# One trunk step with mLSTM and band attention: whole conditioning rows at the start, another order in the first MLP's last group, and head groups one after the other in attention

## The chip, the cores and the metric

The kernel runs on one core of a Trainium2 chip. The metric is the device time of one execution in microseconds (us). TensorE (PE) multiplies matrices, VectorE (DVE) and ScalarE (ACT) do elementwise work, GpSimd (POOL) a little, and SyncE (SP) issues every DMA. Each engine works through its own queue in order.

## The reference

The step has two layers over 1056 tokens: 1024 of a prompt and 32 of a second sequence, each with its own conditioning vector c. Layer 0 is an mLSTM mixer and an MLP with squared ReLU, layer 1 is band attention (own chunk of 64 tokens and 8 chunks before it, or 512 cached keys for the second sequence) and such an MLP. Ahead of each mixer and each MLP the stream is scaled and shifted by values that come from c:

```python
sh1, sc1, g1, sh2, sc2, g2 = jnp.split(ada_mod(c, p['w_ada'][l], p['b_ada'][l])[:, None, :], 6, axis=-1)
u = x * (1 + sc1) + sh1
...
kv = (x * (1 + kv_scale) + kv_shift) @ p['w_kv']
q = (u @ p['w_q_b'][lb]).reshape(Bsz, S, NH_B, HD_B)
...
y = o @ p['w_out_b'][lb]
x = layer_norm(ALPHA * x + (1 + g1) * y, p['ln_g'][l, 0], p['ln_b'][l, 0])
u = x * (1 + sc2) + sh2
f = jnp.square(jax.nn.relu(u @ p['w_up'][l])) @ p['w_down'][l]
x = layer_norm(ALPHA * x + (1 + g2) * f, p['ln_g'][l, 1], p['ln_b'][l, 1])
```

Here ada_mod is silu(c) @ w + b, the width is 1024 and that of the MLP 4096. All values are 32-bit floats.

## The kernel before

**Products.** The stream lies in SBUF with features on partitions, eight chunks (k = 0 to 7) of 128 features, and in three token blocks TBS: block 0 (tokens 0 to 383), block 1 (384 to 767) and block 2 (768 to 1055, whose last 32 are the second sequence). A product of two fp32 matrices is made of three matmuls on halves that add up to the operand: high by high, high by low, low by high (proj, lines 118 to 120; for v lines 455 to 457). Each operand is therefore split: for weights, a copy on ACT makes the high half and a subtraction on DVE the low one (split, lines 89 and 90); for the scaled stream U (u in layer 1's MLP), modulate makes the high half on ACT (L324), the same value unrounded on DVE or ACT (L326, L328), and the low half on DVE (L329).

**Buffers and order.** Raw weights are loaded into a ring of three buffers (tag raw), their halves lie in six (tag wc); a buffer is used anew when its readers are done. PSUM has eight banks. A scheduler of the framework places each engine's instructions; small generators (Flow) are advanced one step at a tick, and the code says after which product a step is due. In attention PE's order is the code's own (manual_schedule). Each engine then keeps that order, waiting where an operand is missing.

**The start.** The 8 rows (k) of 128 by 2048 of w_ada that give shift and scale of layer 0 are loaded in quarters (q) of 512 columns: first quarters 0 and 2 of all k (ada_start(0)), which hold what chunks 0 to 3 need, later 1 and 3. Two matmuls for each k put their 32 output rows on partitions 32q. Each half ends with copies (sada), transposes (adat) and an addition (ada). x is transposed on PE (xps), U is made from PSUM, and x is copied to xt and stored (xsp). v's product begins with chunks 0 to 3 of block 0, stops for the second half of the conditioning, and goes on; qk follows.

**MLP.** w_up and w_down go in 8 groups g of 512 hidden features. up(g, c, ti) is one product of 128 hidden features c and block ti (24 matmuls), down(g, w, fc, block) one of 128 output features (12 matmuls), added to acc by DVE (add_gated). In the last group g = 7 all ups stand ahead of all downs; then the downs go block by block, and behind each block its layer norm is started: sums on DVE, sr on ACT, mean_n and var_n as matmuls on PE, the new U. In layer 0 q's product comes next, then kv.

**kv and attention.** Ahead of the first kv token block the four blocks of 128 cached keys are loaded, copied twice side by side (kd_c) and transposed (kt_c). uk is the scaled stream for kv. Attention works on units (gp, c): head group pair gp of 2 and chunk c, wide ones (chunks 8 to 15) and slim ones in turn, and the two gp in turn. PE makes scores (s), DVE their maxima (mx), ACT the exponentials (p), PE their transposes (pt, pT) and the sums (pv), which become QO.

**After attention.** open_acc loads the stream back into three accumulators acc, gain_shift scales it (L893, 24 times on ACT), and out_proj (op_b) multiplies QO by w_out's halves w_ob: first output columns pr 0 for blocks 2, 1, 0, then pr 1 to 3. The norms of the blocks are due after so many ticks (W10), and MLP 1 follows.

Of the kernel before, what the change touches and what calls it, by code (L numbers as in the profile page):

```python
# [75 lines left out]
def trunk_kernel(ctx: ExitStack, tc: tile.TileContext, a, o):  # L76
# [116 lines left out]
    def ada_load(k, q, mk):  # L193
        raw = mk([P, 512], f"rada_0_{k}_{q}")
        nc.sync.dma_start(raw, a["w_ada"][0, k * P:(k + 1) * P, q * 512:(q + 1) * 512])
        return raw
    PRE = 3
    pre = {(k, q): ada_load(k, q, wc_tile) for k, q in ((0, 0), (0, 2), (1, 0), (1, 2))[:PRE]}
    c_rows = raw_tile([16, P], "c_rows")
    nc.sync.dma_start(c_rows[0:8], a["c_prompt"].rearrange("b (k p) -> (b k) p", p=P))  # L200
    nc.sync.dma_start(c_rows[8:16], a["c_sample"].rearrange("b (k p) -> (b k) p", p=P))
    tp = tpt("tp_c")
# [128 lines left out]
    START = 5  # L331
# [35 lines left out]
    def x_block(t0, n, load=True):  # L367
        if load:
            x_load(t0, n)
        for k in range(KC):  # L370
            ps = tpt(f"xps_{t0}_{k}")
            for i in range(0, n, P):
                xr = xrows[t0, i]
                m = xr.shape[0]
                nc.tensor.transpose(ps[:, i:i + m], xr[:, k * P:(k + 1) * P], ident[:m, :m])
# [4 lines left out]
            nc.scalar.copy(xt[:, k, t0:t0 + n], ps[:, :n])  # L380
            yield
        nc.sync.dma_start(xsp[0][:, :, t0:t0 + n], xt[:, :, t0:t0 + n])

    start_tile = rot([(raw_tile, 3), (wc_tile, 4), (y_tile, 1), (rc_tile, 1)])

    def ada_start(half):

        ps = adat(f"ada_0{half}")
        for k in range(KC):
            for q in (half, half + 2):  # L390
                raw = pre.pop((k, q), None) or ada_load(k, q, start_tile)
# [18 lines left out]
    for i in range(START):  # L410
        flow.tick()
# [287 lines left out]
    def after_v0(t):  # L699
# [4 lines left out]
        elif t == 5:  # L704
            flow.finish(xa[2])
# [728 lines left out]
```

## Time and profile before

| | us |
|---|---|
| median of three runs (lowest 2531.4, highest 2533.92) | 2532.17 |
| the profiled execution | 2531.46 |
| its span in the profile | 2529.6 |

Places in the trace by PE's rows: the start with v to 86.6, qk, mLSTM and the output gate to 435, op_a to 532, the first MLP to 1279, q to 1380, kv to 1442, attention to 1647, op_b to 1760, the second MLP to 2517. A row of waits names the engine, the line that waited, what it waited for, the total, the times and the longest. In rows of instructions, "out<-in" are the program's names, followed by the shape, and brackets give the idle time just before. A matmul's own time overlaps that of its neighbours: the distance of two starts is what one costs. A row of stretches gives busy time of each engine, the granted share of the PE clock, the mean share of the DMA engines that was busy, and GB/s.

### The profile page before, as it was taken

Reading aid. Unit: us, or ns where it says so; the run is one execution under the profiler, and the core shown is the slowest. Engines: PE = TensorE matmul, PEld = TensorE weight load, DVE = VectorE, ACT = ScalarE, POOL = GpSimd, SP = SyncE. Lnnn points to the kernel's source line nnn. Section 1 sums busy time; section 2 is a strip of 40 time slices with the busy share of each in tenths; the row PEclk is TensorE's granted clock in tenths of the full one; section 3 lists DMA queues with packets and bytes.
Section 4 is the critical chain, followed back from the end, with each engine's and each line's share of the span. In section 5 each row is a group of like instructions: output and inputs, shape, how many; then the busy total and the mean of one; then the engine's idle time right before and its main releaser. Section 6 shows DMA issues by size and latency. Waiting matters only on the chain.

```text
span 2529.6 us, 39897 instructions
## 1 busy us (share of the span) xinstructions
PE 2466.1 (97%) x15784; PEld 2356.0 (93%) x15784; DVE 1677.0 (66%) x3851; ACT 953.2 (38%) x2023; POOL 165.8 (7%) x315
## 2 busy tenths in 40 slices
PE   7999999999999999999999899989999999999998
PEld 3899999999999999999999877689999999999997
DVE  3899998788678678766597677737634334343337
ACT  3654446383212211221376566637621221221222
POOL 0111100000000000000001144400000000000003
PEclk9999999999999999999999999989999999999999
DMA  7522323413224234223123400051111111111101
GB/s 235 166 89 92 95 80 105 152 34 102 90 85 136 81 94 132 87 90 122 59 84 102 101 1 1 6 156 34 51 51 42 51 43 50 42 59 34 51 26 70
DMA packets 192063, 201.20 MB, mean 80 GB/s; under 512 B 9336, under 2 KB 180748, under 8 KB 191876
## 3 DMA queue, kind: packets, MB, share of 16 engines
q1 hardware_dynamic: 191876, 198.65, 25.4%
q8 instruction: 124, 2.03, 0.3%
q14 instruction: 63, 0.52, 0.1%
HBM read 183.38 MB, written 17.60 MB: 79 GB/s over the span
## 4 chain that ended last, share of the span: by engine, by line
PE 83%; DVE 7%; ACT 3%; DMA 3%; issue 1%; SPq 0%; DVEq 0%; POOL 0%; ACTq 0%
PE dn L118 10%; PE dn L120 10%; PE dn L119 10%; PE up L118 10%; PE up L119 9%; PE up L120 9%; PE pv L1284 2%; PE pt L1264 2%; PE s L1234 2%; DVE ada_room L236 1%; PE q L118 1%; PE q L119 1%; PE q L120 1%; DMA ada_room<-in_w_ada_dram 1%; PE op_a L118 1%; PE op_a L119 1%
## 5 line engine op out<-in xcount | busy, mean ns | idle before, releaser
L118 PE MATMUL dn<-h,w_dn 128*128 128x384 f32 (+2 forms) x1568 | 505.9, 323 | 0.0
L120 PE MATMUL dn<-h,w_dn 128*128 128x384 f32 (+2 forms) x1568 | 502.1, 320 | 0.0
L119 PE MATMUL dn<-h,w_dn 128*128 128x384 f32 (+2 forms) x1568 | 497.8, 317 | 0.0
L959 DVE SCALAR_TENSOR_TENSOR acc<-dn,ada,acc 128x384 f32<-128x384 f32 (+5 forms) x536 | 244.0, 476 | 237.2 <-PE dn L120 235.0
L118 PEld LDWEIGHTS dn<-h,w_dn 128*128 128x128 f32 x1568 | 294.5, 188 | 0.8 <-issue 0.2
L119 PEld LDWEIGHTS dn<-h,w_dn 128*128 128x128 f32 x1568 | 294.3, 188 | 0.1
L120 PEld LDWEIGHTS dn<-h,w_dn 128*128 128x128 f32 x1568 | 294.0, 187 | 0.0
L998 DVE TENSOR_TENSOR r<-r 128x384 f32<-128x384 f32 (+1 forms) x192 | 100.0, 523 | 275.6 <-ACT h L997 275.0
L996 ACT ACTIVATE r<-up 128x384 f32<-128x384 f32 (+1 forms) x192 | 88.5, 462 | 448.0 <-PE up L120 437.2
L118 PE MATMUL up<-U,w_up 128*128 128x384 f32 (+1 forms) x768 | 249.3, 325 | 0.0
L119 PE MATMUL up<-U,w_up 128*128 128x384 f32 (+1 forms) x768 | 248.2, 323 | 0.0
L120 PE MATMUL up<-U,w_up 128*128 128x384 f32 (+1 forms) x768 | 247.4, 322 | 0.0
L118 PE MATMUL up<-u,w_up 128*128 128x384 f32 (+1 forms) x768 | 246.5, 321 | 0.0
L120 PE MATMUL up<-u,w_up 128*128 128x384 f32 (+1 forms) x768 | 246.5, 321 | 0.0
L119 PE MATMUL up<-u,w_up 128*128 128x384 f32 (+1 forms) x768 | 246.4, 321 | 0.0
L89 ACT CAST w_up<-raw_up 128x1024 fp32r<-128x1024 f32 x64 | 66.8, 1048 | 413.1 <-PE dn L120 274.3
L236 DVE SCALAR_TENSOR_TENSOR aacc<-rada,cs,aacc 128x256 f32<-128x256 f32 x448 | 190.4, 478 | 0.0
L118 PEld LDWEIGHTS up<-U,w_up 128*128 128x128 f32 x768 | 144.2, 188 | 0.1
L120 PEld LDWEIGHTS up<-U,w_up 128*128 128x128 f32 x768 | 144.3, 188 | 0.0
L120 PEld LDWEIGHTS up<-u,w_up 128*128 128x128 f32 x768 | 144.2, 188 | 0.0
L119 PEld LDWEIGHTS up<-U,w_up 128*128 128x128 f32 x768 | 144.2, 188 | 0.0
L119 PEld LDWEIGHTS up<-u,w_up 128*128 128x128 f32 x768 | 144.1, 188 | 0.0
(318 smaller groups left out, 5260.5 us busy)
## 6 DMA issues: line engine op xcount, KB each, us to landing
raw_up<-in_w_up_dram SPq DMA_DIRECT2D x64, 512.0 KB
raw_dn<-in_w_down_dram SPq DMA_DIRECT2D x64, 512.0 KB
rada<-in_w_ada_dram SPq DMA_DIRECT2D x48, 512.0 KB
ada_room<-in_w_ada_dram SPq DMA_DIRECT2D x32, 512.0 KB
rada<-in_w_ada_dram SPq DMA_DIRECT2D x32, 256.0 KB
rada<-in_w_ada_kv_dram SPq DMA_DIRECT2D x16, 512.0 KB
acc<-xsp SPq DMA_DIRECT2D x4, 1536.0 KB
rc<-rc_d SPq DMA_DIRECT2D x8, 528.0 KB
```

Of the source, the lines that this page charges most:

```text
L89: nc.scalar.copy(dst_h, src)
L118: nc.tensor.matmul(ps, wh, mov(0, k), start=(k == 0), stop=False)
L119: nc.tensor.matmul(ps, wh, mov(1, k), start=False, stop=False)
L120: nc.tensor.matmul(ps, wl, mov(0, k), start=False, stop=(k == nk - 1))
L236: nc.vector.scalar_tensor_tensor(acc[:, cnd], raw[:, k], sc, acc[:, cnd], op0=ALU.mult, op1=ALU.add)
L959: nc.vector.scalar_tensor_tensor(xs, ps[:, off + o:off + o + mm_], gate[:, fc, cnd:cnd + 1], xs, op0=ALU.mult, op1=ALU.add)
L996: nc.scalar.activation(r, ps[:, :n], AF.Relu)
L998: nc.vector.tensor_mul(r, r, r)
L1234: nc.tensor.matmul(s[:, b, :w], qst, kk[i][:, g, k0 + j0:k0 + j0 + w], start=(i == 0), stop=(i == 1))
L1264: nc.tensor.transpose(pt[:kp, j - j0, pr * P:(pr + 1) * P], ps_[pr][:, j * P:j * P + kp], ident)
L1284: nc.tensor.matmul(pv[64 * e:64 * e + 64, :nq], V[:kp, vt0 + j, g * 64:(g + 1) * 64], pts[e][:kp, j, :nq], start=(j == 0), stop=(j == nt - 1))
```

## The change

Five things are done. At the start, whole rows of w_ada are loaded (two DMAs of 128 x 1024 each into one wc buffer), four matmuls for each k fill all 128 output partitions, and the whole conditioning is finished in one step, ahead of v; U is made from xt in SBUF instead of PSUM; v goes chunk by chunk over the three token tiles of a block, with the next block's transposes and U between, and x is stored after v. In the first MLP's last group, three ups (c = 3 of block 1, c = 2 and 3 of block 2) come after block 0's downs, and the weights of the downs are asked for when the first block needs them. The cached keys go in with kv's token blocks 0, 2, 4 and 6. Attention does all units of gp 0 and then all of gp 1; pr 0's two halves of w_out are loaded and split within gp 1. The accumulators are loaded in the order 2, 1, 0, with two halves of pr 1 and of pr 2 after the first two. In W10 two of the due times grow.

```diff
@@ -190,15 +190,19 @@
...
+    def ada_load(k):
+
+        raw = wc_tile([P, 2 * D], f"rada_0_{k}")
+        for i in range(2):
+            nc.sync.dma_start(raw[:, i * D:(i + 1) * D], a["w_ada"][0, k * P:(k + 1) * P, i * D:(i + 1) * D])
         return raw
-    PRE = 3
...
     c_rows = raw_tile([16, P], "c_rows")
...
+    adaw = [ada_load(k) for k in range(4)]
...
@@ -364,54 +356,46 @@
...
+    def x_transpose(t0, n, eng):
+
...
+            eng[k % len(eng)](xt[:, k, t0:t0 + n], ps[:, :n])
+            yield
+
+    def u_chunks(t0, n):
+        for k in range(KC):
             for off, m, cnd in segs(t0, n):
...
-                modulate(ps[:, off:off + m], m, sc1[:, k, cnd:cnd + 1], sh1[:, k, cnd:cnd + 1],
+                modulate(xt[:, k, t0 + off:t0 + off + m], m, sc1[:, k, cnd:cnd + 1], sh1[:, k, cnd:cnd + 1],
                          uap(0, k, t0 + off, m), uap(1, k, t0 + off, m), tmp[:, :m])
...
+    def ada_mm(k):
+
+        for q in range(4):
+            nc.tensor.matmul(ada_ps[32 * q:32 * q + 32, :512], cs[:, k, :], adaw[k][:, q * 512:(q + 1) * 512],
+                             start=(k == 0), stop=(k == KC - 1))
...
+    def ada_first():
+
+        sb = rc_tile([P, 512], "sada")
+        ps2 = nmt("adat")
+        for hf in range(2):
+            (nc.scalar.copy if hf else nc.vector.tensor_copy)(sb[:, 256 * hf:256 * hf + 256],
+                                                              ada_ps[:, 256 * hf:256 * hf + 256])
+            for b in (2 * hf, 2 * hf + 1):
+                nc.tensor.transpose(ps2[:, b * P:(b + 1) * P], sb[:, b * P:(b + 1) * P], ident)
+        nc.vector.tensor_tensor(
+            ada[:, 0:16, :].rearrange("p (q b) j -> p q b j", q=4),
+            ps2.rearrange("p (b q j) -> p q b j", b=4, q=4)[:, :, :, 0:2],
+            pt2[:, 0:16].rearrange("p (q b) -> p q b", q=4)[:, :, :, None].broadcast_to([P, 4, 4, 2]), op=ALU.add)
...
@@ -434,45 +418,57 @@
...
+    def v_chunk(ps, ws, t, k):
+        w = ws[k // 4]
+        n = w.shape[-1]
+        uh, ul = uap(0, k, t * P, P), uap(1, k, t * P, P)
+        nc.tensor.matmul(ps[:, :n], uh, w[:, 0, k % 4, :], start=(k == 0), stop=False)
+        nc.tensor.matmul(ps[:, :n], uh, w[:, 1, k % 4, :], start=False, stop=False)
+        nc.tensor.matmul(ps[:, :n], ul, w[:, 0, k % 4, :], start=False, stop=(k == KC - 1))
...
+    def v_first(ws, nxt):
+
+
+        vts = []
+        for bi, (t0, n) in enumerate(TBS):
+            ts = range(t0 // P, (t0 + n + P - 1) // P)
+            pss = {t: (mmt, nmt, mmt)[bi % 2 * (t % 2)](f"v_0_{t}") for t in ts}
+            for k in range(KC):
+                for t in ts:
+                    v_chunk(pss[t], ws, t, k)
+                nxt(bi, k)
+            vts += [v_out(pss[t], 0, t) for t in ts]
...
@@ -694,36 +690,40 @@
...
+    xT = [x_transpose(t0, n, (nc.scalar.copy, nc.vector.tensor_copy)[:2 - (i > 0)]) for i, (t0, n) in enumerate(TBS)]
+    uT = [u_chunks(t0, n) for t0, n in TBS]
+    x_load(*TBS[0])
+    adaw += [ada_load(k) for k in (4, 5)]
+    for k in range(4):
+        ada_mm(k)
+    vw = [v_weight(0, 0)]
+    adaw += [ada_load(k) for k in (6, 7)]
+    for k in range(4, 6):
+        ada_mm(k)
+    for _ in xT[0]:
+        pass
+    for k in range(6, 8):
+        ada_mm(k)
+    vw.append(v_weight(0, 1))
+    x_load(*TBS[1], wc_tile)
+    x_load(*TBS[2])
+    ada_first()
+    for _ in uT[0]:
+        pass
+    flow.add(small_params(), SP)
+
+    def next_u(bi, k):
+        if bi < 2:
+            next(xT[bi + 1])
+            next(uT[bi + 1])
+            if k == KC - 1:
+                for g in (xT[bi + 1], uT[bi + 1]):
+                    for _ in g:
+                        pass
...
+    vts = [v_first(vw, next_u)]
+    for t0, n in TBS:
+        nc.sync.dma_start(xsp[0][:, :, t0:t0 + n], xt[:, :, t0:t0 + n])
...
@@ -797,15 +797,17 @@
...
-    def open_acc(l, order):
+    def open_acc(l, order, between=None):
...
-        for ti in order:
+        for ti in order if between is None else reversed(order):
             t0, n = TBS[ti]
             nc.sync.dma_start(accs[ti], xsp[l][:, :, t0:t0 + n])
+            if between:
+                between(ti)
...
@@ -813,7 +815,7 @@
...
-    W10 = (8.0, 8.0, 0.0, 0.0, 0.0, 3.0)
+    W10 = (10.0, 12.0, 0.0, 0.0, 0.0, 3.0)
...
@@ -1027,15 +1029,32 @@
...
                             for ti in order:
                                 down(g, w, fc, *TBS[ti])
-                    for c in range(1, 4):
-                        for ti in order:
-                            up(g + 1, c, ti)
+                    if g < NG - 2 or last is not TBS:
+                        for c in range(1, 4):
+                            for ti in order:
+                                up(g + 1, c, ti)
                 else:
-                    ws = [wblock(f"dn{l}_{g}_{pr}", w_dn, g * 512, pr * 256) for pr in range(4)]
-                    for blk in last:
+                    ws = []
+
+                    def finish(blk):
                         for fc in range(KC):
+                            if len(ws) < 4 and fc % 2 == 0:
+                                ws.append(wblock(f"dn{l}_{g}_{fc // 2}", w_dn, g * 512, fc * P))
                             down(g, ws[fc // 2], fc, *blk)
                         after_tb(blk)
+                    if last is TBS:
+
+                        for c, ti in ((1, 0), (1, 1), (1, 2), (2, 0), (3, 0), (2, 1)):
+                            up(g, c, ti)
+                        finish(last[0])
+                        for c, ti in ((3, 1), (2, 2), (3, 2)):
+                            up(g, c, ti)
+                        rest = last[1:]
+                    else:
+                        ws += [wblock(f"dn{l}_{g}_{pr}", w_dn, g * 512, pr * 256) for pr in range(4)]
+                        rest = last
+                    for blk in rest:
+                        finish(blk)
         return mm, norm, norm_out, out_proj, mlp, gain_shift
 
 
@@ -1169,13 +1188,16 @@
...
-    for t in range(4):
+
+    def cached_keys(t):
         cr = tmp_t([P, 256], f"ck_{t}")
         nc.sync.dma_start(cr, ck[t * P:(t + 1) * P])
-        flow.add(put_keys(cr, P, TP + t * P, f"c{t}"))
-        flow.tick()
         nc.sync.dma_start(V[:, 8 + t], cv[t * P:(t + 1) * P])
+        yield 3.0
+        yield from put_keys(cr, P, TP + t * P, f"c{t}")
     for t in range(NT):
+        if t % 2 == 0 and t < 8:
+            flow.add(cached_keys(t // 2))
...
@@ -1315,24 +1337,39 @@
...
-    wide = [(gp, c) for c in (8, 12, 13, 14, 15, 9, 10, 11) for gp in range(2)]
-    slim = [(gp, c) for c in (7, 6, 5, 4, 16, 3, 2, 1, 0) for gp in range(2)]
-    units = []
-    for i in range(18):
-        units += wide[i:i + 1] + slim[i:i + 1]
...
+    def wo_block(pr, half):
+        cols = wo[:, 256 * pr:256 * pr + 256]
+        return wtile(f"ob{pr}_{half}", lambda raw: [
...
+    wide, slim = (8, 12, 13, 14, 15, 9, 10, 11), ((7, 6, 5, 4, 16, 3, 2, 1, 0), (16, 7, 6, 5, 4, 3, 2, 1, 0))
     with tc.manual_schedule(engines={mybir.EngineType.PE}):
-        for gp, c in units:
-            for e in range(2):
-                flow.add(att_group(gp, c, e))
-                flow.tick()
+        for gp in range(2):
+            for i in range(17):
+                c = slim[gp][i // 2] if i % 2 else wide[i // 2] if i < 16 else slim[gp][8]
+                for e in range(2):
+                    flow.add(att_group(gp, c, e))
+                    flow.tick()
+                if gp and i in (8, 11):
+                    wo_pre[0, len(wo_pre)] = wo_block(0, len(wo_pre))
         flow.finish()
     psT_cm.__exit__(None, None, None)
     at_cm.__exit__(None, None, None)
...
+    def more_wo(ti):
+
+        if ti:
+            for half in range(2):
+                wo_pre[3 - ti, half] = wo_block(3 - ti, half)
+    accs_cm, acc = open_acc(1, fwd, more_wo)
```

In the first place, SP's queue at the start, rada is a piece of w_ada, xr a piece of x with tokens on partitions, and raw_v a half of v's weights. Before, from the second place on:

```order
L195 DMA rada_4_0_150<-in_w_ada_dram 128x512
L364 DMA xr_256_160<-in_x_prompt_dram 128x1024
L195 DMA rada_5_0_162<-in_w_ada_dram 128x512
L195 DMA rada_5_2_165<-in_w_ada_dram 128x512
L195 DMA rada_6_0_168<-in_w_ada_dram 128x512
L195 DMA rada_6_2_171<-in_w_ada_dram 128x512
L195 DMA rada_7_0_174<-in_w_ada_dram 128x512
L195 DMA rada_7_2_177<-in_w_ada_dram 128x512
L96 DMA raw_v_0_201<-in_w_in_a_dram 128x4x256
L96 DMA raw_v_0_201<-in_w_in_a_dram 128x4x8
L195 DMA rada_1_1_232<-in_w_ada_dram 128x512
L195 DMA rada_2_1_247<-in_w_ada_dram 128x512
```

and in the changed kernel, from its fifth place on:

```order
L197 DMA rada_0_102<-in_w_ada_dram 128x1024 x2
L197 DMA rada_1_105<-in_w_ada_dram 128x1024 x2
L197 DMA rada_2_108<-in_w_ada_dram 128x1024 x2
L197 DMA rada_3_111<-in_w_ada_dram 128x1024 x2
L356 DMA xr_0_145<-in_x_prompt_dram 128x1024
L356 DMA xr_128_147<-in_x_prompt_dram 128x1024
L356 DMA xr_256_149<-in_x_prompt_dram 128x1024
L197 DMA rada_4_151<-in_w_ada_dram 128x1024 x2
L197 DMA rada_5_154<-in_w_ada_dram 128x1024 x2
L96 DMA raw_v_0_173<-in_w_in_a_dram 128x4x256
L96 DMA raw_v_0_173<-in_w_in_a_dram 128x4x8
L96 DMA raw_v_1_241<-in_w_in_a_dram 128x4x256
```

The quarters 1 and 3 of all rows, which stood behind v's first weights, are gone; whole rows stand first, block 0's x behind four of them, and both halves of v's weights ahead of the last two rows.

In the second place, DVE's queue at the end of the first MLP, dn_7_fc_t0 is the down product of feature chunk fc and the block that begins at token t0, s_n_0 and sr_n_0 are block 0's sums for its norm, r and h the squares of an up. Before:

```order
L959 SCALAR_TENSOR_TENSOR acc_0_5312<-dn_7_6_0_12846,ada,acc_0_5312 128x384
L959 SCALAR_TENSOR_TENSOR acc_0_5312<-dn_7_7_0_12860,ada,acc_0_5312 128x384
L847 TENSOR_TENSOR s_n_0_12874<-s_n_0_12874,acc_0_5312 128x768
L848 TENSOR_TENSOR s_n_0_12874<-s_n_0_12874 128x384
L959 SCALAR_TENSOR_TENSOR acc_1_5308<-dn_7_0_384_12882,ada,acc_1_5308 128x384
L90 TENSOR_TENSOR sr_n_0_12879<-s_n_0_12874,sr_n_0_12879 128x384
L959 SCALAR_TENSOR_TENSOR acc_1_5308<-dn_7_1_384_12896,ada,acc_1_5308 128x384
L959 SCALAR_TENSOR_TENSOR acc_1_5308<-dn_7_2_384_12910,ada,acc_1_5308 128x384
L855 TENSOR_TENSOR acc_0_5312<-acc_0_5312,mean_n_0_12924 128x768 x4
```

Now:

```order
L961 SCALAR_TENSOR_TENSOR acc_0_5251<-dn_7_6_0_12695,ada,acc_0_5251 128x384
L961 SCALAR_TENSOR_TENSOR acc_0_5251<-dn_7_7_0_12709,ada,acc_0_5251 128x384
L849 TENSOR_TENSOR s_n_0_12723<-s_n_0_12723,acc_0_5251 128x768
L850 TENSOR_TENSOR s_n_0_12723<-s_n_0_12723 128x384
L90 TENSOR_TENSOR sr_n_0_12728<-s_n_0_12723,sr_n_0_12728 128x384
L1000 TENSOR_TENSOR r_7_3_384_12756<-r_7_3_384_12756 128x384
L1001 TENSOR_TENSOR h_7_3_12555<-r_7_3_384_12756,h_7_3_12555 128x384
L857 TENSOR_TENSOR acc_0_5251<-acc_0_5251,mean_n_0_12791 128x768
L1000 TENSOR_TENSOR r_7_2_768_12786<-r_7_2_768_12786 128x288
```

Behind block 0's last downs stood block 1's downs; now the squares of ups of blocks 1 and 2 stand there, and the norm of block 0 begins ahead of them.

In the third place, ACT's queue between attention and op_b, w_ob_i is the high half of a weight half i of w_out, QO and pT belong to attention, and acc_ti is block ti's accumulator. Before:

```order
L1289 CAST QO_13257<-pv_0_17595 128x256
L89 CAST w_ob_0_17653<-raw_ob_0_17650 128x1024
L893 ACTIVATE acc_0_17615<-acc_0_17615,pt_83 128x384 x8
L893 ACTIVATE acc_1_17611<-acc_1_17611,pt_83 128x384 x6
L893 ACTIVATE acc_2_17607<-acc_2_17607,pt_83 128x288 x8
L893 ACTIVATE acc_1_17611<-acc_1_17611,pt_83 128x384 x2
L89 CAST w_ob_1_17659<-raw_ob_1_17656 128x1024
L89 CAST w_ob_0_17823<-raw_ob_0_17820 128x1024
L89 CAST w_ob_1_17829<-raw_ob_1_17826 128x1024
```

Now (w_ob of pr 0 stands 66 and 43 rows ahead of this, between the exponentials of attention):

```order
L1311 CAST QO_13196<-pv_0_17546 128x256
L89 CAST w_ob_0_17571<-raw_ob_0_17568 128x1024
L895 ACTIVATE acc_2_17558<-acc_2_17558,pt_83 128x288 x4
L89 CAST w_ob_1_17577<-raw_ob_1_17574 128x1024
L895 ACTIVATE acc_2_17558<-acc_2_17558,pt_83 128x288 x4
L895 ACTIVATE acc_1_17562<-acc_1_17562,pt_83 128x384 x6
L89 CAST w_ob_0_17584<-raw_ob_0_17581 128x1024
L895 ACTIVATE acc_1_17562<-acc_1_17562,pt_83 128x384 x2
L89 CAST w_ob_1_17590<-raw_ob_1_17587 128x1024
L895 ACTIVATE acc_0_17566<-acc_0_17566,pt_83 128x384 x8
L89 CAST w_ob_0_17786<-raw_ob_0_17783 128x1024
```

The second half of the first weights stood behind 24 scalings; now both are split within attention, and the next two pairs stand between the scalings, which begin with block 2.

More of the change, by code (lines that the diff above doesn't have):

```diff
@@ L379, in x_block @@
                          uap(0, k, t0 + off, m), uap(1, k, t0 + off, m), tmp[:, :m])
-            nc.scalar.copy(xt[:, k, t0:t0 + n], ps[:, :n])
             yield
[L382 to L391, printed above, removed]
-                nc.tensor.matmul(ps[32 * q:32 * q + 32, :512], cs[:, k, :], raw[:, :512],
-                                 start=(k == 0), stop=(k == KC - 1))
-            yield
-        sb = rc_tile([P, 512], f"sada_0{half}")
-        ps2 = nmt(f"adat_0{half}")
-        for i, q in enumerate((half, half + 2)):
-            rows = slice(32 * q, 32 * q + 32)
-            (nc.scalar.copy if i else nc.vector.tensor_copy)(sb[rows], ps[rows, :512])
-            for b in range(4):
-                nc.tensor.transpose(ps2[:, i * P + b * 32:i * P + b * 32 + 32], sb[rows, b * P:(b + 1) * P],
-                                    ident[rows, rows])
-            nc.vector.tensor_tensor(
-                ada[:, 4 * q:4 * q + 4, :], ps2[:, i * P:(i + 1) * P].rearrange("p (b j) -> p b j", b=4)[:, :, 0:2],
-                pt2[:, 4 * q:4 * q + 4][:, :, None].broadcast_to([P, 4, 2]), op=ALU.add)
-        ap = ada[:, KC + 4 * half:KC + 4 * half + 4, :]
-        nc.vector.tensor_scalar_add(ap, ap, 1.0)
@@ L409, in trunk_kernel @@
-    ag = flow.add(ada_start(0))
-    for i in range(START):
-        flow.tick()
-    x_load(*TBS[0])
-    flow.finish(ag)
-    xg = [x_block(t0, n, t0 == TBS[2][0]) for t0, n in TBS]
+    ada_ps = adat("ada_0")
+    def ada_mm(k):
[14 more added lines that the diff above has]
+            pt2[:, 0:16].rearrange("p (q b) -> p q b", q=4)[:, :, :, None].broadcast_to([P, 4, 4, 2]), op=ALU.add)
@@ new lines, in v_out, with v_proj @@
+    def v_out(ps, h, t):
+        m = P if t < NT - 1 else TS
+        vt = A.tile([P, 258], F32, tag="vt", name=f"vt_{h}_{t}", bufs=9)
+        nc.scalar.copy(vt[:m, :256], ps[:m, :256])
+        nc.gpsimd.memset(vt[:m, 256:258], 1.0)
+        if h == 0:
+            nc.vector.tensor_copy(bass.AP(g64.tensor, g64[:m, t, 0:4].offset, [g64[:m].ap[0], [32, 2], [1, 4]]),
+                                  ps[:m, 256:264].rearrange("p (a b) -> p a b", a=2))
+        return vt
+    def v_proj(h, after):
+        ws = [v_weight(h, half) for half in range(2)]
+        vts = []
+        for t in range(NT):
+            ps = mmt(f"v_{h}_{t}")
+            for k in range(KC):
+                v_chunk(ps, ws, t, k)
+            vts.append(v_out(ps, h, t))
+            after(t)
+        return vts
@@ L1348, in trunk_kernel, with wo_get @@
     mm, norm, norm_out, out_proj, mlp, gain_shift = make_layer(acc, lambda name: psD.tile([P, 512], F32, tag="mm", name=name, bufs=8), u2ap)
[L1349 to L1355 removed]
+    def wo_get(pr, half):
+        return wo_pre.pop((pr, half), None) or wo_block(pr, half)
     def o_mov(hl, k, ti):
```

106 lines of the change are left out of this document (19 added, 87 removed).

## The prediction

> **What bounds the kernel now.** I read the page first (shares, the chain that ended last), then TensorE's waits, then stretches of the places that the change touches, then single rows there.
>
> ```profile
> span 2529.6 us, 39897 instructions
> PE 2466.1 (97%) x15784; PEld 2356.0 (93%) x15784; DVE 1677.0 (66%) x3851; ACT 953.2 (38%) x2023; POOL 165.8 (7%) x315
> PE 83%; DVE 7%; ACT 3%; DMA 3%; issue 1%; SPq 0%; DVEq 0%; POOL 0%; ACTq 0%
> ```
>
> TensorE (PE) is busy 97% of the span and carries 83% of the chain. The change keeps nearly every matmul, so it can win only PE's idle 63 us and busy time that isn't full-rate work: half clock, or a paced start. The waits of PE at the places touched:
>
> ```profile
> PE op_b L118 <- ACT w_ob L89: 6.4, 2, 5.0
> PE var_n L842 <- ACT qr_n L89: 2.9, 2, 2.0
> PE q L118 <- DVE QO L1119: 2.0, 1, 2.0
> PE kt_c L1141 <- DVE kd_c L1136: 1.8, 2, 1.3
> PE q L118 <- ACT U L324: 1.8, 2, 1.2
> PE kt_c L1141 <- ACT kd_c L1135: 1.4, 2, 1.0
> PE mean_n L842 <- ACT sr_n L89: 1.2, 1, 1.2
> PE q L119 <- DVE U L329: 0.4, 1, 0.4
> ```
>
> Columns: total wait, times, longest. Together 17.9 us; no single one is large. The start, by stretches (PE, PEld, DVE, ACT, POOL busy; granted clock, DMA share, GB/s), and rows that give prices:
>
> ```profile
> 0.00:20.00 20.00, 12.41 (x37) 3.19 (x38) 1.84 (x12) 2.14 (x5) 1.05 (x8) 1.00 0.84 292
> 20.00:40.00 20.00, 16.46 (x69) 7.01 (x67) 6.84 (x13) 6.03 (x10) 0.00 (x0) 0.91 0.81 264
> 40.00:60.00 20.00, 16.41 (x96) 11.20 (x94) 9.65 (x21) 9.55 (x19) 0.23 (x5) 0.91 0.44 146
> GB/s 37 327 262 233 337 406 411 389 202 279 208 301 320 371 225 252 206 172 0 0 23 332 354 28 0 312 370 215 344 2 250 335 264 305 294 215 271 171 34 345
> L392 PE MATMUL ada<-rada,cs 128*32 128x512 f32 x64 | 25.0, 739 | 2.9 <-DMA rada<-in_w_ada_dram 1.9 <-DVE cs L213 1.1
> 21.45 0.68 DVE L399 COPY sada<-ada 32x512 f32<-32x512 f32 x1 [14.05 <-PE ada L392]
> 24.00 1.23 ACT L324 ACTIVATE U<-xps,ada 128x384 fp32r<-128x384 f32 x2
> 24.72 0.64 PE L455 MATMUL v<-w_v,U 128*128 128x264 f32 x3 [1.35 <-ACT U L324]
> 34.13 0.28 PE L457 MATMUL v<-w_v,U 128*128 128x264 f32 x1
> 34.25 0.29 PE L455 MATMUL v<-w_v,U 128*128 128x264 f32 x1
> 41.74 0.71 PE L375 MATMUL xps<-ident,xr 128*128 128x128 f32 x5
> 86.62 0.42 PE L118 MATMUL qk<-U,w_qk 128*128 128x384 f32 x1
> ```
>
> (The GB/s row is of the first 90 us in 40 slices of 2.25.) For 60 us PE looks 75% busy while few matmuls run: 64 conditioning matmuls with 32 output rows, then only two abreast, hold it 25.0 us, trickling in behind their loads. v runs at a matmul each 0.12 us (34.13 to 34.25), yet its 216, 26 us of work, are spread from 24.72 until qk begins at 86.62. The first stage is thus bound by the order of loads and by PE taking conditioning rows singly in the middle of v.
>
> **The start (after: all conditioning rows first, four matmuls abreast, then v without breaks).** Ahead of v must land 8 rows of 1.05 MB, the first x block (1.57 MB) and v's weights (1.08): 11.04 MB. Before moved that much in its first 40 us (20 x 292 + 20 x 264 kB), while SP also waited for buffers. Unhindered slices reach 389 to 411 GB/s. I take 380, since rows are now 4 KB long and six wide buffers stand ready, from 4 us on (four small loads are issued first): last row in at 4 + 29 = 33 us. Bounds: 31 (411), 46 (264). The last four matmuls take about 1.5 us, the copy, transposes and addition about 2.2 (21.45 to 24.00 is 2.55 with more steps), first U to first v 0.7: v starts at about 37.5. PE then has 26.6 us of v, 48 transposes of blocks 1 and 2 at 0.13 (41.74, five in 0.64) = 6, one half-clock window 1.7 (below), and about 1 of waiting: qk at about 73 instead of 86.62. The copies and splits of U hide under this only just:
>
> ```profile
> L324 ACT ACTIVATE U<-xps,ada 128x384 fp32r<-128x384 f32 x16 | 10.6, 672 | 7.0 <-PE xps L375 5.7 <-DVE ada L407 1.0
> L380 ACT COPY xt<-xps 128x384 f32<-128x384 f32 x16 | 7.6, 478 | 2.7 <-DVE utmp L326 2.5
> ```
>
> ACT needs 1.15 us per full chunk, PE 1.1 (nine matmuls) plus 0.4 of transposes; were the cover short, it would cost 2 to 4 us. **-13.5; bounds -17 and -1** (landing at 46). The xsp stores go behind v in SP's queue, ahead of qk's first weights, which are due 20 us later: nothing. Row first: 389 to 411 GB/s in slices here. The Trainium skill ("DMA: Bandwidth & Descriptors", Bandwidth) names about 358 GB/s per core as what binds loads from HBM; this trace passes it, and by that rule the landing would be at about 35 us by its figure, an estimate, and the term -11.5.
>
> **The first MLP's last group (three ups moved between block 0's and block 1's downs).** Stretches around the end of the MLP and in q:
>
> ```profile
> 1240.00:1250.00 10.00, 10.00 (x59) 10.00 (x58) 5.40 (x8) 0.00 (x0) 0.00 (x0) 1.00 0.01 2
> 1250.00:1260.00 10.00, 10.00 (x59) 10.00 (x58) 7.56 (x11) 3.61 (x5) 0.00 (x0) 1.00 0.00 0
> 1260.00:1280.00 20.00, 20.00 (x139) 20.00 (x139) 19.54 (x35) 9.52 (x16) 0.00 (x0) 1.00 0.09 27
> 1310.00:1315.00 5.00, 2.39 (x11) 1.78 (x10) 4.84 (x8) 4.91 (x10) 0.00 (x0) 0.87 0.47 173
> 1315.00:1320.00 5.00, 5.00 (x25) 5.00 (x24) 3.82 (x8) 4.97 (x9) 0.00 (x0) 0.79 0.41 145
> ...
> 1303.79 0.34 PE L118 MATMUL q<-U,w_q 128*128 128x384 f32 x1
> 1303.96 0.34 PE L119 MATMUL q<-U,w_q 128*128 128x384 f32 x1
> ...
> L998 DVE TENSOR_TENSOR r<-r 128x384 f32<-128x384 f32 (+1 forms) x192 | 100.0, 523 | 275.6 <-ACT h L997 275.0
> ```
>
> From 1260 VectorE (DVE) has no gap left (19.54 of 20): norm steps of three blocks, q's weights and evictions stand in one queue. PE runs dry only at its far end, 1306 to 1314, and not for one reason: the three q rows add up to 4.2 us of waiting for U's halves and for an eviction (QO) behind them. Then comes a slow clock: 0.87 and 0.79 in two stretches of 5 us is (0.13 + 0.21) x 5 = 1.7 us less. Three ups are 72 matmuls, 24 of 384 columns at 0.17 (1303.79 to 1303.96) and 48 of 288, by columns 0.13: 10.3 us. Block 0's norm begins that much earlier against PE's remaining work, at the place where DVE has 4.6 + 2.4 = 7 us of gaps; but the ups' own two DVE steps of about 0.5 us each (L998 and its successor) now come behind it, 3 us. So DVE gets through about 7 us sooner, which is more than PE waited; U's and QO's waits shrink first, and the norm's mean and var matmuls, placed with one to two groups more ahead of them, are late next. SP asks for dn_7's weights pair by pair now, so a late one could stop PE in block 0. **-5; bounds -6 and 0.**
>
> **Cached keys spread over kv.** In the kv start PE waits 1.8 + 1.4 for the duplicated cached keys; each of the four pairs of transposes now stands between two kv blocks, its two loads on SP issued with it in mind and its copies 3 ticks ahead, so that the copies need not all be made before the first product. What kv's own inputs (uk) cost DVE stays, and some of the wait may pass to them. **-3; bounds -3.5 (all, and a little clock) and 0** (all passed on).
>
> **Attention in pairs, w_out weights ahead, accumulators in reverse.** ACT in the seam:
>
> ```profile
> 1647.12 1.05 ACT L89 CAST w_ob<-raw_ob 128x1024 fp32r<-128x1024 f32 x1
> 1652.14 13.85 ACT L893 ACTIVATE acc<-acc,pt 128x384 f32<-128x384 f32 x24 [3.97 <-DMA acc<-xsp]
> 1665.89 2.92 ACT L89 CAST w_ob<-raw_ob 128x1024 fp32r<-128x1024 f32 x3
> 1645.00:1650.00 5.00, 3.59 (x11) 2.35 (x11) 1.65 (x2) 1.68 (x3) 0.00 (x0) 0.50 1.08 279
> 1665.00:1670.00 5.00, 3.03 (x11) 2.80 (x11) 3.05 (x3) 3.81 (x5) 0.00 (x0) 0.52 0.07 11
> ```
>
> The second half-weight's cast stands behind 24 scalings that first wait for acc: PE loses 6.4, and twice runs at half clock; 3 to 4 us of that are lost too. (0.50 on 3.59 busy and 0.52 on 3.03 is 1.8 and 1.5 us.) After, two halves are cast inside attention and the next four between scalings; acc's blocks are loaded in the order in which op_b uses them, the small one first, each followed by a pair of weight loads on SP. The scalings are hidden behind op_b's first products, whose evictions alone need them; block 2's eight are the first. Were acc late, PE would stop when its eight PSUM banks are full. All of the wait and half of the clock loss goes: **-8; bounds -10 and -5** (the first wait, 1.4, stays or comes back as a full bank).
>
> In attention, the row maxima (mx) that DVE makes are what PE waits for most, and two casts of weights come on top:
>
> ```profile
> PE s L1234 <- DVE mx L1245: 7.2, 15, 3.0
> L90 DVE TENSOR_TENSOR w_qk<-raw_qk,w_qk 128x1024 fp32r<-128x1024 f32 x4 | 4.8, 1221 | 0.2 <-ACT w_qk L89 0.2
> ```
>
> Two splits cost ACT 2 x 1.05 and DVE 2 x 1.22; if neither is hidden, mx is late by the 2.4 and p by part of the 2.1, +3.5 together. The head groups in sequence instead of in turn change which wide and slim units stand side by side; no row tells with what effect, so I bound it by a gain of less than half of the 7.2, -3. **+1; bounds -3 and +3.5**, nearer to the casts, whose price a row has.
>
> **Norms of layer 1 (W10).** mean and var matmuls wait 4.1 in all at op_b's end; var of the first block and mean and var of the second now stand one product (24 matmuls, some 4 us) further from what they need, the first mean does not; but the ups that follow stand closer behind the last var, and w_up's casts, two of 1.05, come among the norms' steps on ACT, so the first up can be late instead. **-1.5; bounds -4 and +2.**
>
> Sum: -13.5 - 5 - 3 - 8 + 1 - 1.5 = -30. The profiled execution took 2531.46, 0.7 under the median 2532.17; against the median this is **2502 us**. About 0.2% (5 us) is what a measurement can tell from no change.
>
> **Rivals.** (1) *Loads land late*: at 264 GB/s (the second stretch) v starts at about 50, the term falls to -1: 2514 to 2515. For it: the same queue, rows still waiting for a buffer; against it: DMA share 0.81 in that stretch, so 326 at full share. (2) *Waits only move*: DVE stays saturated in q and op_b's norms wait elsewhere, so the MLP, keys and norm terms vanish: -13.5 - 8 + 1, 2512. For it: DVE's 19.54 of 20 and nothing taken off its list. Against it: the 7 us of gaps just ahead. (3) *Slower*: rows hold SP's queue for buffers that PE frees in order, as 40 to 60 us shows at 146 GB/s. Then 11.04 MB take 76 us, v starts at 84 instead of 37.5: +33 against -16.5 elsewhere, 2549. It decides once the last row lands after 63 us, under 187 GB/s. Against it: four rows fit at once and PE has nothing else ahead. (4) *PE stays at half clock through v*, each chunk waiting for its U: 26.6 + 6 us double instead of one window, +31 - 30: about 2533, no change. Against it: q's clock is down for 10 us at most after 4.2 us of waiting, and v ran at 0.12 a matmul with waits between (34.13). The Trainium skill ("TensorE: Matmul & The Clock Gate", Part 1) says that an idle window of about 3.4 us halves the clock and a busy one restores it; the 1310 and 1315 rows, 1.7 us lost, agree with one such window. By that rule v would start cold here, for one window if it has no breaks (as in the sum) and for all of it if every window held enough of them.
>
> **Chances.** Forecast 0.57, (1) 0.16, (2) 0.20, (3) 0.03, (4) 0.04. Faster: the first three, 0.93; same 0.04; slower 0.03. Range 2488 to 2520: below, all terms at their good ends (-17 - 6 - 3.5 - 10 - 3 - 4 = -43.5) would be 2489; above, rivals (1) and (2) lie at 2512 to 2515, both together at 2524, of which I take in most. The forecast's own range is 2493 to 2509.
>
> **What would show it.** Right: qk's first matmul at 71 to 75 us; DMA above 350 GB/s until 33 us, no conditioning matmul amid v; no wait of q for QO or U, DVE busier from 1240 to 1260 relative to that end; no op_b wait for w_ob; kt_c waits under 1. Wrong: PE's clock at 0.5 beyond one window after 37 us; U's splits ending v's waits; p or mx waits grown in attention behind w_ob's casts; new mean or var waits after op_b; a dn_7 wait for weights.

## The result, and the profile after

The changed kernel took 2510.35 us (median of four runs, 2506.05 to 2511.88) against 2531.78 for the kernel before on the same chip: ratio 0.9913, 95% interval 0.9896 to 0.993, so 21 us faster. Forecast were 2502, with a range of 2488 to 2520 and a narrower one of 2493 to 2509 for the forecast's own mechanism. Three executions of this study, two of the kernel before and one of a variant, took 4001 to 5567 us and are left out of every ratio. From the page of the changed kernel:

```profile
span 2508.4 us, 39863 instructions
PE 2454.0 (98%) x15772; PEld 2352.9 (94%) x15772; DVE 1668.5 (67%) x3850; ACT 949.3 (38%) x2018; POOL 167.6 (7%) x315
PE 83%; DVE 7%; DMA 3%; ACT 2%; issue 1%; POOL 0%; SPq 0%; DVEq 0%; ACTq 0%; POOLq 0%
```

PE's idle time is 54 us instead of 63; the other 12 us came off its busy time, nearly all of it in the start (to the first qk matmul PE was busy for 70.8 us before and for 58.1 now). Its waits after the change, at the places that the prediction named:

```profile
PE ada L383 <- DMA rada<-in_w_ada_dram: 6.5, 5, 3.6
PE s L1256 <- DVE mx L1267: 6.5, 14, 2.4
PE kv L1209 <- DVE uk L90: 4.3, 3, 3.3
PE var_n L844 <- ACT qr_n L89: 2.0, 1, 2.0
PE mean_n L844 <- ACT sr_n L89: 0.8, 1, 0.8
PE up L120 <- DVE w_up L90: 0.8, 1, 0.8
PE q L118 <- DVE QO L1138: 0.5, 1, 0.5
PE q L118 <- ACT U L326: 0.2, 1, 0.2
```

The waits of op_b for w_ob (6.4) and of kt_c for kd_c (3.2) are gone and q's are down from 4.2 to 0.7. Two rows are new: kv waits 4.3 us for uk, and up 0.8 us for the split of its weights, as the prediction feared for the first up. The start, by the same stretches as before, and the first matmuls of v and qk:

```profile
0.00:20.00 20.00, 11.65 (x40) 2.34 (x40) 2.07 (x14) 2.42 (x6) 1.18 (x12) 1.00 0.84 322
20.00:40.00 20.00, 14.70 (x83) 7.03 (x84) 9.36 (x18) 8.25 (x14) 0.00 (x0) 0.91 1.03 374
40.00:60.00 20.00, 20.00 (x153) 18.24 (x152) 16.91 (x51) 16.39 (x39) 0.29 (x4) 1.00 0.60 192
36.66 0.39 PE L435 MATMUL v<-w_v,U 128*128 128x264 f32 x1 [0.86 <-ACT U L326]
71.77 0.42 PE L118 MATMUL qk<-U,w_qk 128*128 128x384 f32 x1
```

Loads run at 322 and 374 GB/s (292 and 264 before), v begins at 36.66, and after the 0.86 us of idle time just before it PE has no gap up to 60. To follow the difference on its way to the end, here are the first matmuls of later stages, of before and then of the changed kernel:

```profile
1279.37 0.34 PE L118 MATMUL q<-U,w_q 128*128 128x384 f32 x1
1379.87 0.38 PE L1141 MATMUL kt_c<-ident,kd_c 128*128 128x128 f32 x2
1441.61 0.40 PE L1234 MATMUL s<-k,QO 128*128 128x288 f32 x1
1648.22 0.64 PE L118 MATMUL op_b<-QO,w_ob 128*128 128x320 f32 x1 [1.41 <-ACT w_ob L89]
2469.29 0.38 PE L918 MATMUL yt<-ident,acc 128*128 128x128 f32 x2
```

```profile
1265.48 0.34 PE L118 MATMUL q<-U,w_q 128*128 128x384 f32 x1
1361.19 0.28 PE L1207 MATMUL kv<-w_kv,uk 128*128 128x256 f32 x1
1426.49 0.53 PE L1256 MATMUL s<-k,QO 128*128 128x288 f32 x2
1632.82 0.41 PE L118 MATMUL op_b<-QO,w_ob 128*128 128x320 f32 x1
2447.72 0.49 PE L920 MATMUL yt<-ident,acc 128*128 128x128 f32 x3
```

The distance of two such rows is a stage (yt is the first transpose of the output). With the first down of the second MLP (1819.2 before, 1794.2 after) they give:

| stage | before | after | difference | forecast |
|---|---|---|---|---|
| to the first qk | 86.6 | 71.8 | -14.8 | -13.5 |
| qk to q | 1192.8 | 1193.7 | +1.0 | 0 |
| q | 100.5 | 95.7 | -4.8 | -5 |
| kv | 61.7 | 65.3 | +3.6 | -3 |
| attention | 206.6 | 206.3 | -0.3 | +1 |
| op_b to the first down of MLP 1 | 171.0 | 161.4 | -9.6 | -8 - 1.5 |
| from there to yt | 650.1 | 653.5 | +3.4 | 0 |
| the rest | 60.3 | 60.7 | +0.4 | 0 |

Four rows hold within 1.5 us. Two do not: kv got longer instead of shorter, and the second MLP, which the change doesn't touch, lost 3.4 us.

Each number of this table comes from one execution of each kernel, and not every stage repeats to a microsecond. In the kernels of this study that have the old last group, q took 99.3 us in five and 100.5 in one; with the old op_b, the stretch to the first down took 170.4 to 174.2. The times of kv and attention vary most, as shown below.

### The profile page after: what moved, and what is told of

Its sections match the earlier page's. It is cut to its first block, busy times and chain, and to the rows that moved or that the text cites. A ratio compares the mean times of both kernels' runs of the same rounds, so it can differ in the third digit from the quotient of the medians.

```text
span 2508.4 us, 39863 instructions
## 1 busy us (share of the span) xinstructions
PE 2454.0 (98%) x15772; PEld 2352.9 (94%) x15772; DVE 1668.5 (67%) x3850; ACT 949.3 (38%) x2018; POOL 167.6 (7%) x315
## 4 chain that ended last, share of the span: by engine, by line
PE 83%; DVE 7%; DMA 3%; ACT 2%; issue 1%; POOL 0%; SPq 0%; DVEq 0%; ACTq 0%; POOLq 0%
PE dn L119 10%; PE dn L118 10%; PE up L118 10%; PE dn L120 10%; PE up L120 10%; PE up L119 10%; PE pv L1306 2%; PE pt L1286 2%; PE s L1256 2%; PE op_b L118 1%; PE op_b L119 1%; PE op_b L120 1%; DMA ada_room<-in_w_ada_dram 1%; DVE ada_room L238 1%; PE o L118 1%; PE o L120 1%
## 5 line engine op out<-in xcount | busy, mean ns | idle before, releaser
L1000 DVE TENSOR_TENSOR r<-r 128x384 f32<-128x384 f32 (+1 forms) x192 | 100.2, 524 | 279.2 <-ACT h L999 278.8
```

Of the source, the lines that this page charges most:

```text
L1000: nc.vector.tensor_mul(r, r, r)
```

## The experiments

There are three main questions: is the start's gain its own, why did kv not get shorter, and where do the 3.4 us of the second MLP come from. Each run has its own runs of the kernel before on the same chip (medians 2531.2, 2533.7 and 2533.0 for the three groups of four); the stages come from one profiled execution each. Where two variants ran on different chips, their ratios are what can be compared.

**The start alone** (of the diff, the parts from ada_load to the xsp stores, in the kernel before).

> The kernel before with the new start alone (whole conditioning rows, v without breaks). Theory: the start's gain is its own and is carried to the end unchanged, since qk begins 14.8 us sooner in the changed kernel and nothing behind it depends on absolute time: first qk matmul at about 71.8 us, every later mark 14 to 15 us sooner, time 2517 (ratio 0.994). Rival: part of it is given back where the work behind was paced by loads that start no sooner: first q matmul less than 13 us sooner, time over 2519.

2521.7 us, ratio 0.9961 (0.9946 to 0.9976). The first qk matmul stood at 71.8, op_b began at 1633.8, still 14.4 sooner, and yt at 2460.7, only 8.6 sooner: the start keeps its gain up to op_b and 5.8 us are lost behind it, 3.5 of them again between the first down of MLP 1 and yt (653.6 instead of 650.1). The rival's bound (over 2519) was passed, but not for its reason: the first q stood 15.9 us sooner.

**The first MLP's last group alone.**

> The kernel before with the new last group of the first MLP alone. Theory 1 (the parts are separate): q takes 95.7 instead of 100.5 us and the kv stage stays at 61.7, so 4 us in all, 2528. Theory 2 (VectorE owes the work, the wait only moves from q to kv): q takes 95.7, but kv grows to about 65, so about 1 us in all, 2531.

2527.75, ratio 0.9984 (0.9975 to 0.9994). q took 95.8 us and kv 61.8: the wait in q goes and doesn't come back in kv. This is theory 1.

**The cached keys alone, and all but them.**

> The kernel before with the cached keys spread alone. Theory 1 (the transposes of the cached keys at kv's start covered the late input halves uk; spread, they cover nothing): PE's waits for kd_c go, waits for uk of about 4 us come, kv takes about 65 instead of 61.7 us, time 2535. Theory 2 (VectorE's debt from q is what shows in kv): kv takes 58 to 59, time 2529.

> The changed kernel with the cached keys as before. Theory 1: kv takes 60 to 62 us with short waits for kd_c, time 3 to 4 us under the changed kernel's 2510.35, 2507. Theory 2: kv stays at 64 to 66, time 2510.

Spread alone: 2534.86, ratio 1.0015 (1.0006 to 1.0025), 3.6 us slower. The kd_c waits went, waits of 2.2 us for uk came, kv took 62.1 and attention 208.9. Without them in the changed kernel: 2504.65, ratio 0.9895 (0.9879 to 0.9911); kv 63.5, attention 203.5. The interval of that ratio overlaps the changed kernel's, so the second run alone wouldn't show a price; the two together point to one of some 4 to 5 us. But the size that theory 1 gave to kv alone is wrong: kv grew by 0.4 us and not by 3.

**What the price consists of.** In three profiled executions with the changed kernel's code of kv and attention, kv took 62.0, 62.9 and 65.3 us and attention 210.2, 208.3 and 206.3: where one is long the other is short, and the two together take 271 to 272. Here are the stretches of kv and of attention's first 20 us, in the changed kernel, in the kernel with the old due times (below), which has the same code here, and in the changed kernel without spread keys:

```profile
1361.19:1426.49 65.30, 60.89 (x486) 60.03 (x485) 43.08 (x80) 34.76 (x88) 11.54 (x6) 0.95 0.33 87
1426.49:1446.49 20.00, 14.16 (x82) 10.32 (x83) 12.57 (x42) 10.64 (x28) 7.18 (x11) 0.91 0.61 135
```

```profile
1361.08:1423.12 62.04, 58.55 (x486) 57.49 (x484) 42.99 (x80) 34.49 (x88) 12.08 (x6) 1.00 0.34 92
1423.12:1443.12 20.00, 14.39 (x56) 11.14 (x58) 11.35 (x37) 9.30 (x24) 5.68 (x8) 0.60 0.60 135
```

```profile
1361.32:1424.78 63.46, 58.87 (x487) 57.40 (x485) 46.89 (x80) 34.48 (x85) 10.60 (x6) 1.00 0.33 86
1424.78:1444.78 20.00, 15.22 (x102) 11.39 (x100) 14.00 (x46) 12.24 (x33) 7.59 (x14) 1.00 0.57 133
```

Call the missing clock of a stretch its length times one minus the granted share. It is 3.3 + 1.8 us in the first, 0 + 8.0 in the second and nothing in the third, where kv and attention together take 267.0 us. PE's waits in kv don't explain the difference: 4.3 and 3.3 us for uk in the first two, and 2.0 + 1.4 for kd_c and 1.3 for uk in the third. So the waits for kd_c were replaced by waits for uk of about the same size, which is why nothing was won, and what made it worse is half clock, now in kv and now in attention. The mean clock of whole executions says the same: 0.9938 over the four of the changed kernel against 0.996 over the four without spread keys, 0.9898 over ten with the keys spread alone against 0.9916 over eighteen of the kernel before. That is 5.6 and 4.5 us of missing clock, estimates from shares on record to 0.001, against 4.6 and 3.8 us of time by the ratios. Why the clock falls more often there is not shown.

**What makes uk late.** In the changed kernel's trace, the engines around the longest wait of kv:

```profile
1373.50 1.22 DVE L90 TENSOR_TENSOR uk<-x,uk 128x1024 fp32r<-128x1024 f32 x1
1374.25 1.05 ACT L89 CAST uk<-x 128x1024 fp32r<-128x1024 f32 x1
1374.75 0.53 SPq L1180 DMA_DIRECT2D x<-xsp  x1
1380.61 1.90 POOL L1185 TENSOR_TENSOR x<-x,kvss 128x1024 f32<-128x1024 f32 x1 [8.28 <-DMA x<-xsp]
1382.54 1.22 DVE L1186 TENSOR_TENSOR x<-x,kvss 128x1024 f32<-128x1024 f32 x1 [5.73 <-POOL x L1185]
1383.68 1.22 DVE L90 TENSOR_TENSOR uk<-x,uk 128x1024 fp32r<-128x1024 f32 x1
1384.96 0.58 PE L1209 MATMUL kv<-w_kv,uk 128*128 128x256 f32 x1 [3.31 <-DVE uk L90]
```

ACT has the high half of a uk at 1375.3. Its low half stands in DVE's queue behind the addition for a block two further on; that one waits for GpSimd, GpSimd for a load, and the load was issued only at 1374.75, just after the split of an earlier block had read its raw buffer to the end (1373.50 + 1.22). DVE idles 5.7 us with the split ready behind the wait. If this is the cause, moving the addition to another engine takes it away:

```diff
-        nc.vector.tensor_add(x, x, kvsh[:, :, cnd:cnd + 1].broadcast_to([P, KC, m]))
+        nc.gpsimd.tensor_add(x, x, kvsh[:, :, cnd:cnd + 1].broadcast_to([P, KC, m]))
```

> The changed kernel with the addition of kv's shift on GpSimd instead of VectorE. In the changed kernel VectorE's queue holds that addition for block t+2 (it waits for a load and GpSimd) ahead of the split of uk for block t, and kv stands 3.3 us for uk. Theory 1a (this wait in VectorE's queue is what makes uk late once the cached keys' transposes no longer fill kv's start): the uk waits of 4.3 us fall under 1.5, kv takes 61 to 62 us instead of 65.3, time 2506. Theory 1b (uk is late because its loads and buffers come late, whichever engine adds): waits for uk stay at 3 us or more, time 2509 to 2511.

2500.95, ratio 0.9868 (0.9849 to 0.9888). All that PE waits for in its kv stage:

```profile
PE kv L1209 <- DVE uk L90: 0.4, 1, 0.4
```

kv took 58.3 us, 3.4 less than before the change: the forecast's -3, once the split no longer stands behind the addition. This is theory 1a, with more gain than it gave (61 to 62 us, 2506). Of the 7.0 us between 65.3 and 58.3, about 3.9 are waits for uk and 3.3 are clock (1.00 in kv, 0.95 without the edit); attention's first 20 us ran at 0.74 in this execution.

> The kernel before with kv's shift added on GpSimd. Theory 1 (the cached keys' transposes at kv's start cover the late uk, so there is little to gain there): kv at 60 to 62 us, time 2529 to 2531. Rival (VectorE's queue delays kv in the kernel before just as much): kv at 58, time 2527.

The same edit in the kernel before: 2532.19, ratio 0.9998 (0.9988 to 1.0007), kv 61.8. There the waits for kd_c stay at 3.4 and nothing is won, as that kernel has no waits for uk that the edit could take away. So the cached keys' copies and transposes at kv's start were both a wait and a cover: the time they took let uk come in time.

**Where the weights lie.** The new start claims a narrow buffer of the ring (raw) before the first wide one (wc), where the kernel before did the opposite. That sets the place of all split weights in SBUF: bytes 18784 and up of each partition instead of 6112 and up (addresses of the two programs); the raw buffers, which no matmul of the MLPs reads, change sides with them, and no other tile in SBUF moves. The first edit gives the changed kernel the old place, the second the kernel before the new one; the order of instructions on every engine stays.

```diff
-        raw = wc_tile([P, 2 * D], f"rada_0_{k}")
+        raw = rada0 if k == 0 else wc_tile([P, 2 * D], f"rada_0_{k}")
...
+    rada0 = wc_tile([P, 2 * D], "rada_0_0")
     c_rows = raw_tile([16, P], "c_rows")
```

```diff
+    c_rows = raw_tile([16, P], "c_rows")
     PRE = 3
...
-    c_rows = raw_tile([16, P], "c_rows")
```

> The changed kernel with one thing altered: the first wide buffer of the ring (tag wc) is claimed ahead of the first narrow one (tag raw), so that the split weights lie at bytes 6112 to 56799 of each partition as they did before the change, and not at 18784 and up; the order of instructions is the same on every engine. The kernel with the new start alone began qk 14.8 us sooner but ended only 8.6 sooner, and its ups of layer 1 over 384 columns come every 175.9 ns instead of 173.45, 3.2 us over 1296. Theory A (the place of the weights in SBUF sets the pace of those matmuls): 173.5 ns again, the second MLP 3.5 us shorter, time 2504 to 2506. Theory B (it is the time at which loads come, or the work of the start that ends up elsewhere): 175.9 ns as in the changed kernel, time 2510.

> The kernel before with the narrow buffers claimed first, so that the weights lie where the changed kernel has them; the order of instructions is the same on every engine. Theory A: ups of layer 1 at 175.9 ns instead of 173.45, the second MLP 3.5 us longer, time 2535 to 2537. Theory B: no difference, 2531.

A third of the ups of layer 1 over 384 columns between the first down and yt (line 118, one of the three of a product), in the kernel before, the changed kernel, the first and the second of these. Behind the bar stand the busy time, which overlaps that of the next matmul, and the mean ns of one:

```profile
L118 PE MATMUL up<-u,w_up 128*128 128x384 f32 x432 | 144.4, 334 | 0.0
```

```profile
L118 PE MATMUL up<-u,w_up 128*128 128x384 f32 x432 | 146.0, 338 | 0.0
```

```profile
L118 PE MATMUL up<-u,w_up 128*128 128x384 f32 x432 | 144.4, 334 | 0.0
```

```profile
L118 PE MATMUL up<-u,w_up 128*128 128x384 f32 x432 | 145.9, 338 | 0.0
```

The pace follows the place and not the kernel: the stretch to yt is 650.1, 653.5, 650.1 and 653.6 us, in this order, and over all runs of this study 650.1 in the eight kernels with the old place and 653.5 or 653.6 in the six with the new one. Over all 1296 ups of this shape the pace is one each 173.45 or 175.9 ns, which makes 3.2 us; the rest is in the other matmuls. The kernel before with the new place is slower in time too, 2535.99 against 2533.7, ratio 1.001 (1.0001 to 1.002). The changed kernel with the old place came to 2506.99 (ratio 0.989, 0.9871 to 0.9909), 3.4 us less, but this interval overlaps the changed kernel's, so there it is the stage that shows it. This is theory A. It explains 3.5 us of what the start alone lost behind op_b; the other 2 lie between op_b and the first down (173.3 instead of 171.0), within what that stretch varies.

**The due times of op_b's norms** (W10 back to 8, 8).

> The changed kernel with the due times of op_b's norms as before the change (8, 8 instead of 10, 12). Theory: the later due times take away about 1.5 us of waiting for mean and var, so 2512. Rival: they only push the first up back, and the time is 2510 or less.

2505.2 (2505.02 to 2509.95), ratio 0.9891 (0.9872 to 0.991): not slower than the changed kernel, so the theory's 2512 is out, and the time is that of the rival. The first up, though, isn't pushed back: with the new due times the first up comes sooner (97.7 us after op_b's first matmul, against 100.2 with the old ones), and the ups then wait (63.6 us from there to the first down, against 60.7). From op_b's first matmul to yt it took 814.5 us, the changed kernel 814.9, with 3.4 us of half clock at op_b's start that the other doesn't have; the changed kernel without spread keys, which has the new due times and no half clock there, took 813.5. So the due times mainly move waits, and whether they are worth nothing or 1 us can't be told from this. The 5 us in time go with the clock of whole executions: the profiled one, at 0.993, took 2509.95, and the other three, at 0.996 and 0.997, took 2505; the changed kernel's four stand at 0.992 to 0.995.

**The order of the head groups alone**, in the kernel before.

> The kernel before with the head group pairs of attention one after the other, and nothing else. Theory: their order makes no difference in attention itself, 205 to 208 us against 206.6, time 2530 to 2532. Rival: it costs or brings over 2 us by another row of wide and slim units, which the weights ahead then hide or spoil.

2533.3, ratio 1.0002 (0.9993 to 1.0012), attention 207.1 us: no difference.

**Both mended, with and without spread keys.**

> The changed kernel with kv's shift added on GpSimd and the split weights back at their old place in SBUF. Theory: the two gains are separate: kv at 58 to 59 us, ups of layer 1 with a median of 173 ns, time 2497 to 2499. Rival: kv's gain moves into attention's start once the rest is faster, 2501 or more.

> The same two edits, but the cached keys at kv's start as before the change. Theory: with uk no longer late, spreading the keys is worth what the prediction said, so without it the waits for kd_c, 3.2 us, stay, kv takes 61 to 62 us and the time is about 3 us more than with spread keys, 2500 to 2502. Rival: spread keys also burden attention's start, which was 3 us shorter without them, so the two are equal, 2497 to 2499.

2502.7 (ratio 0.9878, 0.9863 to 0.9892) and 2501.38 (0.987, 0.9856 to 0.9885), so the first is its rival in time (2501 or more), and the second is its rival in that the two are equal, though not at 2497 to 2499. With spread keys kv takes 58.3 and attention 208.2, without them 62.7 and 203.5: what kv wins, attention's start gives back. (The profiled execution of the second is its fastest, 2496.61 at a clock of 0.997. Over its four executions the clock is 0.9958, over the four with spread keys 0.9938, an estimate of 5 us of missing clock.) The first 20 us of attention, with spread keys and then without:

```profile
1419.10:1429.10 10.00, 6.55 (x25) 4.95 (x26) 6.89 (x24) 4.91 (x15) 2.19 (x3) 0.69 0.88 195
1429.10:1439.10 10.00, 8.34 (x45) 6.44 (x43) 4.85 (x16) 5.08 (x12) 3.60 (x6) 0.63 0.36 74
```

```profile
1420.60:1430.60 10.00, 6.24 (x35) 4.57 (x34) 6.19 (x24) 5.79 (x17) 3.71 (x6) 1.00 0.96 218
1430.60:1440.60 10.00, 8.86 (x66) 6.78 (x66) 7.63 (x23) 6.22 (x16) 3.92 (x9) 1.00 0.23 50
```

The granted clock is 0.69 and 0.63 in the one, 1.00 in the other, and PE gets through 70 instead of 101 matmuls. That is 3.1 + 3.7 us of missing clock, 13.6 us at half speed. The Trainium skill ("TensorE: Matmul & The Clock Gate", Part 1) has the clock halved after an idle window of about 3.4 us and counts windows that run on freely; 13.6 is four of them. But PE's longest single wait in these 20 us was 2.0 us (for mx), so no whole window was idle here, and the trace decides: shorter waits can be enough. That the few waits for k and pT at this point decide it is argued, not shown. The old place of the weights is worth 3.4 us in the second MLP here too (650.1 against 653.5), but the total is no lower than with the addition alone; the mean clock of its four executions is 0.9938 against 0.9945, an estimate of 2 us of the missing 3.4, and the rest is open. So the best of these, 2501 to 2503, can't be told from each other; by their ratios all are some 9 to 11 us faster than the changed kernel.

## Why the prediction was right, and where it was not

- **The total**: 2510.35 lies in the stated range, but just outside the 2493 to 2509 given to the forecast's own mechanism, and nearer to rival 2 (2512) than to 2502. Of the three terms that rival 2 let vanish, the keys' did and more, the due times' may have, and the last group's didn't. That the time lies in the wide range is owed to its covering the rivals' times as well.
- **The start** was right in mechanism and size: -14.8 against -13.5. v began at 36.66 (forecast 37.5), qk at 71.77 (73). The loads ran at 374 GB/s in the second stretch, near the 380 taken. The half-clock window that was counted into v fell on the conditioning matmuls ahead of it (0.91 from 20 to 40 us, 1.00 after). Even so v's stage took 35.1 us, and the sum had 35.3 with the window's 1.7: its other work was summed about 1.5 us too short, and the two errors cancel. The figure of about 358 GB/s that the prediction quotes from the Trainium skill ("DMA: Bandwidth & Descriptors", Bandwidth) was passed again. Rivals 1, 3 and 4 are out.
- **The last group** was right: q -4.8 against -5. Alone it brought 3.5 us in runs and in q, from the 99.3 that q takes in most kernels with the old group. Rival 2 (waits only move) is out for this term.
- **The cached keys** are the step that failed. That "some of the wait may pass to them" stood as the bad end of the range, 0; measured were +3.6 in kv's trace and 3.6 us in time when done alone (there with little of it in kv). I priced the wait removed and did not ask what the removed work had covered: the queue of DVE with an addition that waits for a load, ahead of the split that PE needs. So 2.2 to 4.3 us of waits for uk took the place of 3.2 for kd_c, which is the bad end. Beyond it go 4 to 6 us of half clock, for which the sum had no term. The sum of 3.2 us of waits was right as a prize, as the addition on GpSimd shows, but half clock in attention's start takes it again.
- **op_b and its norms**: -9.6 against -9.5, all w_ob waits gone. That the sum agrees so well is luck. With the old due times op_b alone brought -10.1 where -8 was forecast: its granted clock went from 0.96 over 171.0 us (6.8 us of missing clock, of which the prediction knew 3 to 4 and took half) to 1.00. The new due times brought nothing that shows, where -1.5 was forecast.
- **Attention**: -0.3 against +1; the order of the pairs by itself makes no difference. The agreement is in part luck too, as the stage holds whatever half clock the execution has: with kv it took 271.6 us, and 267.0 without spread keys. There attention was 3.1 us shorter than before, so no price of the casts of w_ob is seen.
- **Left out altogether**: the place of the weights in SBUF, +3.4. It is in no instruction's order, and the trace of before could not show it.

The forecast was 30 us of gain against 21; the keys (6.6) and the weights' place (3.4) are 10 of it, and the start, 1.3 better, the other way; the rest nearly cancels.

## What to carry to other kernels

A wait that is taken away by moving work leaves a hole where the work was: look which operand was coming in under it, and follow that operand's queue back to its load. In an in-order queue, an instruction that waits for a far load must not stand ahead of one that the bottleneck needs next; putting it on an engine that may wait is cheap (GpSimd is busy for 7% of the span here). Before a stage's microseconds are given a cause, look at the granted clock in it: kv took 62.0 to 65.3 us with the same code. And when a change claims buffers in another order, compare where the operands lie before looking for a cause in the schedule.

## What was not expected of the hardware

With the same instructions in the same order, 1296 matmuls of 384 columns came every 173.45 or 175.9 ns (334 or 338 ns in their own rows), by the place of the stationary operand's buffers in SBUF; the moving operand lay in the same place. Other matmuls of the same shape (the ups of layer 0, with another moving operand) kept theirs within 0.3 us over 1536 of them. Which property of the address decides was not tried.

Half clock came in pieces of 3.4 us and multiples of that (28.90 to 32.31 in the changed kernel, 1422.85 to 1436.51 in the one with both mended), each piece 1.7 us of missing clock. In attention's start it came without any single wait as long as a piece.
